# Half-matrix swaps by DMA alone: each engine's rows are regrouped from every sixteenth row to sixteen neighbouring rows, and half rows become whole rows in two pieces

## The chip, the cores and the metric

The kernel runs on one core of one Trainium2 chip. The metric is the device time of one execution in microseconds (us), lower is better. The computation uses no compute engine at all: everything is done by the core's 16 DMA engines, which copy from DRAM to DRAM.

## The reference

```python
x = np.random.randn(8192, 8192).astype(np.float32)

def reference(x):
    return np.fft.ifftshift(x)
```

For an even-sized matrix this exchanges the four quadrants diagonally: output row r, left half, is input row (r + 4096) mod 8192, right half, and output row r, right half, is the left half of that same input row. Each row is 32 KB, each half row 16 KB. The input holds 268.4 MB and so does the output; nothing is computed.

## The kernel before

Two engines issue DMAs, SyncE (`nc.sync`, SP in the profile) and ScalarE (`nc.scalar`, ACT in the profile); each has a DMA queue of its own, called q1 and q10 in the profile. Both queues feed the same 16 DMA engines.

`copy(queue, row, h, step)` at L25 to L32 issues one DMA of 256 half rows (4 MB) at L29. It fills the half of the output rows that starts at column `h` from the other half of the input rows that lie 4096 rows away. The list `dims` has three levels: 16 entries that are one row (32 KB) apart, then 16 entries that are 16 rows (512 KB) apart, then the 4096 neighbouring numbers of a half row. The outermost level is what the 16 DMA engines divide among themselves, so engine e takes rows e, e + 16, e + 32 and so on of the block of 256. At any one moment, if the engines keep step, they work on 16 neighbouring rows; call the number of the step within the DMA j (0 to 15), so that a row of the block is 16 j + e.

The loop at L36 to L39 walks over the output in groups of 1024 rows, four blocks of 256. SP takes the left output halves of blocks 0, 1, 2, 3 and ACT takes the right output halves of blocks 2, 3, 0, 1. That makes 64 DMAs, 32 on each queue. No DMA depends on another's data. The framework gives the DMAs eight completion semaphores in rotation, four for each queue, so each queue has four DMAs under way and its fifth waits for its first to land, and so on.

Of the kernel before, what the change touches and what calls it, by code (L numbers as in the profile page):

```python
# [1 line left out]

# [4 lines left out]


ENGINES = 16


@with_exitstack
def kernel(
    ctx: ExitStack,
    tc: tile.TileContext,
    x: bass.AP,
    out: bass.AP,
):
    nc = tc.nc
    R, C = x.shape  # L20
    hr = R // 2
    hc = C // 2
    per = 16
    rows = ENGINES * per

    def copy(queue, row, h, step):

        dims = [[C, ENGINES], [step * C, per], [1, hc]]
        queue.dma_start(  # L29
            out=bass.AP(out.tensor, out.offset + row * C + h, dims),  # L30
            in_=bass.AP(x.tensor, x.offset + (row + hr) % R * C + hc - h, dims),
        )  # L32

    for first in range(0, R, 4 * rows):  # L36
        for n in range(4):
            copy(nc.sync, first + n * rows, 0, ENGINES)
            copy(nc.scalar, first + (n + 2) % 4 * rows, hc, ENGINES)  # L39


# [1 line left out]
_INS = ['x']  # L43
_OUTS = [((8192, 8192), 'float32')]


def kernel(**inputs):
    import numpy as _np
    import concourse.bacc as _bacc
    import concourse.tile as _tile  # L50
    from concourse import mybir as _mybir
    from concourse.bass_utils import run_bass_kernel_spmd as _run

    nc = _bacc.Bacc("TRN2", target_bir_lowering=False, num_devices=1)  # L54
    arrays, args = {}, []
    for name in _INS:
        a = _np.ascontiguousarray(inputs[name])
        if a.dtype.kind in "iu":
            a = a.astype(_np.int64)
        arrays[f"in_{name}_dram"] = a  # L60
        args.append(nc.dram_tensor(f"in_{name}_dram", a.shape, _mybir.dt.from_np(a.dtype), kind="ExternalInput").ap())
    for i, (shape, dtype) in enumerate(_OUTS):
        dt = _mybir.dt.from_np(_np.dtype(dtype))
        args.append(nc.dram_tensor(f"out_{i}_dram", shape, dt, kind="ExternalOutput").ap())
    with _tile.TileContext(nc) as tc:
        kernel(tc, *args)
    r = _run(nc, [arrays], core_ids=[0])
    got = tuple(r.results[0][f"out_{i}_dram"] for i in range(len(_OUTS)))
    return got[0]
```

## Time and profile before

| quantity | value |
|---|---|
| median of 3 runs | 821.14 us (821.09 to 824.2) |
| span of the profiled execution, first to last instruction | 812.4 us |
| median less span (launch and end, outside the span) | 8.7 us |
| DMAs | 64 of 4096 KB, 32 on SP, 32 on ACT |
| DMA packets | 17408, of which 16384 carry 16 KB each and 1024 carry 4 bytes (completion counts) |
| bytes moved | 268.44 MB read and 268.44 MB written, 330 GB/s one way |

The page states no separate total for the profiled execution beside its span; the runs' times are about 8.7 us above the span. A packet is one contiguous piece moved by one DMA engine. "Landing" is the moment at which the last of a DMA's 16 completion counts arrives. A DMA share of 1.00 means that all 16 engines have a packet under way the whole time.

### The profile page before, as it was taken

What the parts mean: (1) busy time and instruction counts of PE and PEld (TensorE: products, weight loads), DVE (VectorE), ACT (ScalarE), POOL (GpSimd) and SP (SyncE); (2) the same over time, 40 slices, a digit from 0 to 9 for tenths busy, and PEclk for the clock granted to TensorE, in tenths of its full rate; (3) what the DMA queues carried; (4) which work ended last, traced back from release to release, by engine and by line L of the source; (5) the groups of instructions that cost most, each with busy time, mean ns of one, the idle gap of its engine ahead of it and who ended that gap; (6) DMA issues with size and microseconds to landing.
All of it is one profiled execution on the core that took longest, in us unless ns stands there. A gap on an engine that the chain in (4) does not pass through costs nothing. (4 is left out here: it accounts for less than half of the span.)

```text
span 812.4 us, 109 instructions
## 1 busy us (share of the span) xinstructions
POOL 0.2 (0%) x4
## 2 busy tenths in 40 slices
POOL 0000000000000000000000000000000000000000
DMA  9999999999999999999999999999999999999998
GB/s 307 331 331 336 335 331 331 335 325 337 334 332 336 331 333 332 334 339 332 332 334 331 329 331 334 332 328 333 330 334 335 334 328 333 332 331 330 338 331 280
DMA packets 17408, 268.44 MB, mean 330 GB/s; under 512 B 1024, under 2 KB 1024, under 8 KB 1024
## 3 DMA queue, kind: packets, MB, share of 16 engines
q1 hardware_dynamic: 8704, 134.22, 49.7%
q10 hardware_dynamic: 8704, 134.22, 49.5%
HBM read 268.44 MB, written 268.44 MB: 661 GB/s over the span
## 5 line engine op out<-in xcount | busy, mean ns | idle before, releaser
L54 POOL MEMSET const-bfloat16-1.0<- 128x1 bf16 x1 | 0.1, 101 | 0.0
L54 POOL MEMSET const-uint8-127<- 128x1 uint8 x1 | 0.1, 101 | 0.0
L54 POOL MEMSET const-float32-0.0<- 128x1 f32 x1 | 0.1, 98 | 0.2 <-issue 0.2
L54 POOL MEMSET const-float32-1.0<- 128x1 f32 x1 | 0.1, 98 | 0.0
## 6 DMA issues: line engine op xcount, KB each, us to landing
out_dram<-in_x_dram SPq DMA_DIRECT2D x32, 4096.0 KB, 101.0
out_dram<-in_x_dram ACTq DMA_DIRECT2D x32, 4096.0 KB, 101.0
```

The costliest lines, as they stand in the source:

```text
L54: nc = _bacc.Bacc("TRN2", target_bir_lowering=False, num_devices=1)
```

## The change

Each DMA now copies 256 whole rows (8 MB) in 16 KB pieces. The innermost two levels are the two halves of a row: on the input side the left half and then the right half, on the output side the right half and then the left half (the step of that level is negative). The outermost level has 256 entries, one row apart; divided among 16 DMA engines, engine e now takes rows 16 e to 16 e + 15 of the block, one after the other. The engines of one DMA are therefore 16 rows (512 KB) apart instead of one row (32 KB). SP takes the even blocks of 256 rows and ACT the odd ones; there are 32 DMAs instead of 64, 16 on each queue.

```diff
-    per = 16
-    rows = ENGINES * per
+    block = 256
 
-    def copy(queue, row, h, step):
-
-        dims = [[C, ENGINES], [step * C, per], [1, hc]]
+    def copy(queue, row):
+        src = x.offset + (row + hr) % R * C
+        dst = out.offset + row * C + hc
         queue.dma_start(
-            out=bass.AP(out.tensor, out.offset + row * C + h, dims),
-            in_=bass.AP(x.tensor, x.offset + (row + hr) % R * C + hc - h, dims),
+            out=bass.AP(out.tensor, dst, [[C, block], [-hc, 2], [1, hc]]),
+            in_=bass.AP(x.tensor, src, [[C, block], [hc, 2], [1, hc]]),
         )
 
-    for first in range(0, R, 4 * rows):
-        for n in range(4):
-            copy(nc.sync, first + n * rows, 0, ENGINES)
-            copy(nc.scalar, first + (n + 2) % 4 * rows, hc, ENGINES)
+    for first in range(0, R, 2 * block):
+        copy(nc.sync, first)
+        copy(nc.scalar, first + block)
```

## The prediction

> **What bounds the kernel now.** I read the page first. Nothing computes, so only its DMA parts matter.
>
> ```profile
> span 812.4 us, 109 instructions
> DMA  9999999999999999999999999999999999999998
> DMA packets 17408, 268.44 MB, mean 330 GB/s; under 512 B 1024, under 2 KB 1024, under 8 KB 1024
> q1 hardware_dynamic: 8704, 134.22, 49.7%
> q10 hardware_dynamic: 8704, 134.22, 49.5%
> HBM read 268.44 MB, written 268.44 MB: 661 GB/s over the span
> ```
>
> The two queues' packets fill 49.7 + 49.5 = 99.2% of 16 engines' time. There is no idle time to recover; a gain must make the pieces themselves shorter. Next, is the issuing of DMAs ever late? The waits of SP's queue, the timeline and the view of the output tensor say:
>
> ```profile
> SPq L29 <- DMA out_dram<-in_x_dram: 689.4, 28, 25.3
> 0.73 708.44 SPq L29 DMA_DIRECT2D out_dram<-in_x_dram  x32
> L29 SPq DMA_DIRECT2D out_dram<-in_x_dram x32: 571/571/652, 0.7 to 708.6; - x32
> DMA to landing us min/median/max: 25.6/101.0/103.4
> ```
>
> SP waits 28 times, that is for all but its first four DMAs, and issues each of the rest when the one four before it has landed. An issue takes 0.57 us and is followed by 101 us of queueing and moving, so four DMAs of 25 us each are always ready. Issue is not on the path. Last the windows view, for the ends:
>
> ```profile
> 0.00:5.00 5.00, 0.20 (x4) 1.00 0.61 210
> 100.00:200.00 100.00, 0.00 (x0) 1.00 1.00 332
> 806.00:809.00 3.00, 0.00 (x0) 1.00 0.95 317
> 809.00:812.40 3.40, 0.00 (x0) 1.00 0.06 24
> ```
>
> Its last two columns are the DMA share and GB/s. The middle is flat; start and end cost about 0.39 x 5.0 = 2.0 us and 0.05 x 3.0 + 0.94 x 3.4 = 3.3 us.
>
> So the time is the number of pieces per engine, 16384 / 16 = 1024, times the mean length of a piece. The trace holds each packet with its queue, start and duration; the mean over the 16384 pieces is 786.5 ns (lowest 608, a quarter of them at 611 or less, median 732, 95th percentile 1152). 1024 x 786.5 ns = 805.4 us; the span has 7.0 us more, of which start and end are 5.3. The median of the runs lies 8.7 us above the span: 805.4 + 7.0 + 8.7 = 821.1.
>
> A piece at 611 ns is 26.8 GB/s; five of the last pieces of all, when few engines are left, take exactly that. It is the pace of an engine that nobody disturbs. The other 175 ns of the mean is paid to the memory side. Hence the question is only whether the new order of addresses raises or lowers the 786.5.
>
> **Two facts from the packet records decide how I answer.** First, the engines keep step. The 16 completion counts of one DMA arrive within 1.1 to 2.8 us of each other in all 64 DMAs, though nothing in the program holds them together within the four DMAs under way. Second, pieces are not alike. I ordered each queue's pieces by start, cut them into DMAs (256) and steps (16), and averaged each step j over the 32 DMAs of the queue. Steps in fours, mean ns of a piece:
>
> ```
>             j 0-3    j 4-7    j 8-11   j 12-15
> q1          823.5    742.5    846.0    741.0
> q10         818.0    738.5    814.0    769.0
> ```
>
> Steps 0-3 and 8-11 (call their rows A) average 825.4 ns, the others (B) 747.8. The contrast holds in nearly every DMA (mean A less mean B is positive in 31 of 32 on q1 and 28 of 32 on q10). The queues are about three steps apart, so that one is often in A while the other is in B, and the A piece is still the longer one on its own engine. It goes with the piece's own rows, or with its place in its DMA, which here are the same thing: step j is always rows 16 j to 16 j + 15 of a block that starts at a multiple of 256 rows.
>
> **The change part by part.** Bytes, piece size (16 KB) and pieces per engine (1024) stay. Issues fall from 64 to 32: 32 x 0.57 us of queue time go, hidden before under 101 us of DMAs under way, so nothing comes off the time; four DMAs of 8 MB under way are about 202 us of cover. The 4-byte completion packets fall from 1024 to 512; they take 7 ns each, 32 fewer per engine are 0.2 us, which I drop. Left and right half of a row now follow each other on the same queue with one piece of the other queue between. No row of this trace shows such a pair; bounds are the two kinds of steps, 748 and 825 ns a piece (minus 40 to plus 40 us in all). I take zero, since 786.5 is a mean over many neighbourhoods of pieces and lies in the middle, and keep the ends for the range.
>
> The part that I think counts is the division. Before, every engine passed through A and B rows in turn, and so all were equal. After, engine e takes rows 16 e to 16 e + 15 of every block, which is what step j = e was: engines 0-3 and 8-11 get A rows for the whole run, engines 4-7 and 12-15 get B rows. If A rows are slow by their place in memory, the engines drift apart. A B engine ends its 1024 pieces after 1024 x 0.7478 = 765.7 us. By then an A engine has done 765.7 / 0.8254 = 928, and 96 are left. Then eight engines run alone. The low price for their pieces is 611 ns (58.7 us), the high one 825 ns (79.2 us); I take 640 ns, 61.4 us, near the floor, since eight engines at 26.8 GB/s ask for 215 GB/s where the memory side gave 332 all along. Sum: 765.7 + 61.4 + 7.0 + 8.7 = 842.8 us, with ends 840 and 861. The cover allows the drift: over 32 pieces on each of two queues a B engine gains 64 x 78 ns = 5.0 us, over the run 79 us, less than the 202 us of DMAs under way, so B engines needn't wait for A's.
>
> **The rivals.** (1) *No difference.* The contrast belongs to the place in the DMA (say, how descriptors reach an engine), not to the memory. Then every engine has the same mixture after, and the time stays at 821 us, 817 to 825. For it: the contrast has a period of eight steps through all DMAs, whatever the block's higher address bits. Against: queueing that starves an engine should show gaps between packets, and the packets fill 99.2%.
>
> (2) *Slower, and in step.* The engines are now 512 KB apart and keep step, as they did all along; then they lie in the same place of 16 different 512 KB stretches, and if these share banks, every piece pays at least the price of an A piece: 1024 x 0.8254 + 7.0 + 8.7 = 861 us; with the worst single step of the trace, 884 ns (q1, j = 9), 921 us. The same 861 comes out if the coupling that keeps the engines in step makes B engines wait for A's. It decides once the mean piece passes some 790 ns without one half of the engines ending early. For it: the tight step, and 175 ns of memory cost that can grow. Against: at distances of 32 KB the trace shows no such loss for any one engine. The Trainium skill, page "DMA: Bandwidth & Descriptors", section "Latency and other measured facts", has a row on row pitches at large powers of two: copies whose partitions lie 512 KiB apart ran at 207 GB/s per direction, where padded ones reached 214, and 2 MiB apart at 164. That speaks against this change; by 214 / 207 its time would be an estimated 849 us. No run here shows such a distance yet.
>
> (3) *Faster.* Reading a row's two halves one after the other, and spreading the 16 engines over 512 KB stretches, may break up what makes A steps slow, because they no longer meet 15 neighbouring rows of the same kind. If all pieces came at the B price: 1024 x 0.7478 + 7.0 + 8.7 = 781 us; half of that way 801 us. For it: 611 ns is possible and the mean lies 29% above it. Against: the 330 GB/s one way hardly moves in any slice of the run, as from a shared limit that doesn't care for order.
>
> (4) *It isn't what it says.* The compiler could join the two halves of the input row or divide the DMA otherwise. Pieces stay bound by the output side's 16 KB, so I'd expect about no change.
>
> **How the numbers follow.** Drift between A and B engines 0.34 (843 us); slower in step 0.23 (861, up to 921); faster 0.24 (801, down to 781); no difference 0.17, and not what it says 0.02 (821). A change within 0.5% (4 us) can't be told from none here, as the three runs lie 3 us apart. Faster by more: case 3 and a little of case 1, 0.25. Within: most of the cases at 821, 0.16. Slower: 0.59. The likeliest case's own range is 832 to 861, with its low end for a contrast of half the size. The range that holds 8 in 10 leaves out the lower half of case 3 and the upper part of case 2: 796 to 880.
>
> **What would show it.** In the profile after: 32 issues of 8192 KB and 16896 packets (16384 + 512); landing near 202 us. For drift: the 16 completion counts of one DMA spread by 5 us more with each pair of DMAs, to tens of us, while the middle stays at 332 GB/s, and the last 60 us fall to a DMA share near one half and about 215 GB/s. For case 1: spread of a few us and the same 332. For case 2: all slices lower, near 315, ends sharp. For case 3: all slices higher. A spread that stays under 5 us would prove the drift wrong.

## The result and the profile after

The changed kernel takes 872.34 us (median of 4 runs, 869.28 to 875.03) against 821.12 us (4 runs) for the kernel before on the same chip: 1.0617 times as long, 95% interval 1.0587 to 1.0647. The forecast was 843 us. The direction was right; the size was less than half of what came, and the mechanism was another.

The page of the changed kernel, the parts that answer to those shown of before:

```profile
span 868.0 us, 77 instructions
DMA  9999999999999999999999999999999999999998
GB/s 280 316 314 308 309 310 314 313 307 310 308 313 310 313 306 308 313 316 315 302 315 306 310 314 313 314 310 313 316 315 304 312 307 313 316 303 314 313 310 271
DMA packets 16896, 268.44 MB, mean 309 GB/s; under 512 B 512, under 2 KB 512, under 8 KB 512
q10 hardware_dynamic: 8448, 134.22, 49.8%
q1 hardware_dynamic: 8448, 134.22, 49.6%
HBM read 268.44 MB, written 268.44 MB: 618 GB/s over the span
```

The engines are as full as before (49.8 + 49.6 = 99.4%), the bytes are the same, and every one of the 40 slices is lower, 302 to 316 GB/s inside where before had 325 to 339; its line was:

```profile
GB/s 307 331 331 336 335 331 331 335 325 337 334 332 336 331 333 332 334 339 332 332 334 331 329 331 334 332 328 333 330 334 335 334 328 333 332 331 330 338 331 280
```

So each piece takes longer, evenly over the run: the mean of the 16384 pieces is 842.6 ns instead of 786.5. 1024 pieces an engine x 56.1 ns are 57.4 us; the span grew by 55.6 us. No stage and no wait holds the loss.

The waits of SP's queue, its row in the view of the output tensor, and that view's time to landing:

```profile
SPq L32 <- DMA out_dram<-in_x_dram: 140.6, 12, 53.9
L32 SPq DMA_DIRECT2D out_dram<-in_x_dram x16: 555/43842/50152, 0.7 to 648.1; - x16
DMA to landing us min/median/max: 54.1/215.7/218.3
```

An issue now takes a median of 43.8 us where it took 0.57, so there is a visible suspect: the queue seems no longer to accept four DMAs at once. Landing takes 215.7 us, still far more than an issue. The windows view, for the middle and the end (last columns: DMA share, GB/s):

```profile
100.00:200.00 100.00, 0.00 (x0) 1.00 1.00 311
780.00:800.00 20.00, 0.00 (x0) 1.00 1.00 311
860.00:864.00 4.00, 0.00 (x0) 1.00 0.97 295
864.00:868.00 4.00, 0.00 (x0) 1.00 0.45 147
```

The end is sharp: full until 4 us before it. There is no stretch of 60 us at half the engines. The 16 completion counts of each DMA arrive within 0.6 to 1.4 us of each other (before: 1.1 to 2.8). The drift that was forecast didn't happen.

### The profile page after: what moved, and what is told of

Read it like the earlier page. It is cut to its first block, busy times and chain, and to the rows that moved or that the text cites. A ratio compares the mean times of both kernels' runs of the same rounds, so it can differ in the third digit from the quotient of the medians.

```text
span 868.0 us, 77 instructions
## 1 busy us (share of the span) xinstructions
POOL 0.2 (0%) x4
## 2 busy tenths in 40 slices
DMA packets 16896, 268.44 MB, mean 309 GB/s; under 512 B 512, under 2 KB 512, under 8 KB 512
## 3 DMA queue, kind: packets, MB, share of 16 engines
q10 hardware_dynamic: 8448, 134.22, 49.8%
q1 hardware_dynamic: 8448, 134.22, 49.6%
## 6 DMA issues: line engine op xcount, KB each, us to landing
out_dram<-in_x_dram ACTq DMA_DIRECT2D x16, 8192.0 KB, 215.7
out_dram<-in_x_dram SPq DMA_DIRECT2D x16, 8192.0 KB, 215.7
```

## The experiments

Each ratio is to the kernel before on the same chip, with its 95% interval; the kernel before ran at 812.7 to 812.8 us in the first and the last group and at 822.4 to 822.8 us in the others.

**First group: the parts of the change one at a time.** Engines far apart, with all else as before:

```diff
-        dims = [[C, ENGINES], [step * C, per], [1, hc]]
+        dims = [[per * C, ENGINES], [C, per], [1, hc]]
```

> The kernel before (half rows, 64 DMAs of 4 MB, same blocks on the two queues), but each engine takes 16 neighbouring rows, so the engines are 512 KB apart instead of 32 KB. Theory D (distance between engines): about 872 us as in the changed kernel. Theory W (whole rows, left and right in turn on one queue): 821 us. Theory Q (8 MB DMAs, whose issue takes 44 us where it took 0.57 us): 821 us. Theory P (which blocks and halves the two queues work on at the same time): 821 us. If slow rows tied to engines matter by themselves, the 16 completion counts of one DMA spread by tens of us late in the run; if something holds the engines in step, by under 3 us.

Measured: 811.15 us, ratio 0.9985 (0.9963 to 1.0008), completion counts within 0.8 to 2.7 us. Read as it was meant, this acquits the distance; the last group shows that it had not tested it.

The pairing of the queues:

```diff
+    for first in range(0, R, 2 * rows):
+        for h in (hc, 0):
+            copy(nc.sync, first, h)
+            copy(nc.scalar, first + rows, h)
```

> The kernel before, except that SP takes both halves of the even blocks and ACT both halves of the odd ones, in separate 4 MB DMAs, so that both queues copy the same half of rows 256 rows apart at any time, as in the changed kernel. Theory P (pairing of the queues): about 872 us. Theories D, W and Q: 821 us.

Measured: 814.01 us, ratio 1.0011 (0.9987 to 1.0035). At 32 KB distance pairing costs nothing.

Whole rows with the engines near, by making the DMA small:

```diff
-    block = 256
+    block = 16
+    for first in range(0, R, 512):
+        for low in range(0, 256, block):
+            copy(nc.sync, first + low)
+            copy(nc.scalar, first + 256 + low)
```

> The changed kernel with DMAs of 16 rows (512 KB, 512 DMAs) instead of 256: one row an engine, so the engines are 32 KB apart as in the kernel before, while rows are still copied whole, left and right in turn. Theory D: about 821 us, perhaps a few us more for 512 issues. Theory W: 872 us. Theory Q: about 821 us.

Measured: 812.23 us, ratio 0.9996 (0.9978 to 1.0013). Left and right in turn costs nothing at 32 KB distance, nor do 512 issues.

Engines 17 rows apart (`[[C, 16 * 17], [-hc, 2], [1, hc]]`):

> The changed kernel with 17 neighbouring rows an engine instead of 16 (blocks of 272 rows, 30 of them, and two DMAs of 16 rows): the engines are 544 KB apart, which is no power of two. Theory D as a matter of powers of two: the loss goes, 815 to 830 us. Theory D as a matter of distance alone, theories W and Q: 865 to 880 us.

Measured: 841.15 us, ratio 1.0346 (1.0319 to 1.0373), between the two expectations. SP carried 53% of the bytes, so this was repeated evenly later.

**Second group: DMA size, the full queue, or distance and whole rows together (theory DW).**

```diff
f1:  block = 128
f2:  per = 32          # the kernel before, DMAs of 8 MB
f3:  little(queue)     # 16 numbers into SBUF after each big DMA
f4:  for low in range(16): ... [[16 * C, 16], [-hc, 2], [1, hc]]
```

> The changed kernel with DMAs of 128 whole rows (4 MB, 16 pieces an engine) instead of 256: 8 neighbouring rows an engine, engines 256 KB apart. Theory Q (a queue that holds more pieces than fit blocks the issuing engine, as the 44 us issues of the changed kernel show, and pieces then get slower): issues of about 0.6 us, four times 17 descriptors an engine under way as before, ratio to before 1.00. Theory DW (distance and whole rows are each harmless and bad together): ratio 1.04 to 1.06, or less if 256 KB is a better distance than 512 KB.

Measured: 823.09 us, ratio 1.0007 (0.9991 to 1.0023).

> The kernel before with 32 steps in a DMA instead of 16: half rows, engines 32 KB apart, 32 DMAs of 8 MB. Theory Q: issues of some 44 us and ratio 1.05 to 1.06 although order and distance are those of the kernel before. Theory DW: ratio 1.00.

Measured: 823.23 us, ratio 1.0005 (0.9983 to 1.0027).

> The changed kernel with two instead of four big DMAs under way on each queue: a DMA of 16 numbers into SBUF follows each big one and takes every second completion semaphore. Pieces, order and distances are those of the changed kernel, but only 66 descriptors an engine and queue are under way. Theory Q: issues under 1 us and ratio 1.00. Theory DW: ratio 1.06.

Measured: 868.64 us, ratio 1.0554 (1.0519 to 1.0589).

> The changed kernel's order of pieces and distance (whole rows, left and right in turn, engines 512 KB apart) in DMAs of 512 KB: one row of each engine in each. Theory DW: ratio 1.06. Theory Q: ratio 1.00, as the DMAs of 16 neighbouring rows had.

Measured: 872.15 us, ratio 1.0597 (1.0568 to 1.0626).

SP's rows in the view of the output tensor (minimum, median and maximum ns of an issue), of f2, f3 and f4 in this order:

```profile
L28 SPq DMA_DIRECT2D out_dram<-in_x_dram x16: 572/41472/48379, 0.7 to 616.8; - x16
```

```profile
L28 SPq DMA_DIRECT2D out_dram<-in_x_dram x16: 564/565/657, 0.7 to 757.6; - x16
```

```profile
L28 SPq DMA_DIRECT2D out_dram<-in_x_dram x256: 571/571/694, 0.7 to 855.9; - x128
```

This settles the suspect. f2 has issues of 41 us and loses nothing; f3 and f4 have issues of 0.57 us and lose 5.5% and 6.0%. Long issues come with four DMAs of 8 MB on a queue and cost nothing in f2. What the slow ones share is whole rows with engines 512 KB apart; f1, at 256 KB, is not slow. The cleanest pair is e2 and f4: both copy whole rows in 512 DMAs of 512 KB, one row of each engine in each, in blocks of 256 rows dealt to the queues in the same way. They differ only in which 16 rows a DMA takes, neighbours (e2, 0.9996) or rows 512 KB apart (f4, 1.0597).

**Third group: what goes with the distance.** Both queues on the same half, with half rows meant to be far apart; the queues on opposite halves; the queues 16 MB apart; and 1 MB between engines:

```diff
g1:  dims of e1_apart with the loop of e3_blocks
g2:  copy(nc.scalar, first + block, hc)       # ACT: right half of the input first
g3:  copy(nc.scalar, first + (n + 2) * block)
g4:  block = 512
```

> Half rows in 4 MB DMAs, engines 512 KB apart as in e1_apart, but with the blocks of e3_blocks: both queues copy the same half, 256 rows (8 MB) apart. Theory DP (distance and pairing: loss when the pieces of both queues sit at the same place of their 512 KB stretches): ratio 1.06. Theory DW (distance and left-right order within a queue): ratio 1.00.

Measured: 822.2 us, ratio 1.0000 (0.9979 to 1.0022).

> The changed kernel with ACT reading right, then left (and writing left, then right), so that the queues work on opposite halves while engines stay 512 KB apart and rows are whole. Theory DP with the half as part of the place: ratio 1.00. Theory DW: ratio 1.06. Theory DN (the loss needs the queues' blocks to be neighbours, 8 MB apart): ratio 1.06.

Measured: 859.39 us, ratio 1.0437 (1.0401 to 1.0474), 1.8 points less than the changed kernel. That doesn't show what opposite halves are worth, because the two queues came apart here. Their rows in the view of the output tensor:

```profile
L30 ACTq DMA_DIRECT2D out_dram<-in_x_dram x16: 660/47021/83707, 0.7 to 550.4; - x16
L30 SPq DMA_DIRECT2D out_dram<-in_x_dram x16: 554/554/1066, 0.7 to 773.5; - x16
```

ACT issued its last DMA at 550 us, SP at 774; ACT's last piece starts at about 771 us, and SP goes on alone to the end. While the queues still kept step, on opposite halves, the rate was 308 GB/s (10 to 110 us) and 313 GB/s (110 to 220 us); the changed kernel has 310 and 311 in the same stretches. So no gain shows in that part. The record of ACT's DMAs also has another shape, 1 x 512 pieces where SP's have 2 x 256, so that it isn't known which rows ACT's engines took.

> The changed kernel with the two queues 512 rows (16 MB) apart instead of 256, as in the kernel before. Theory DN: ratio 1.00. Theories DP and DW: ratio 1.06.

Measured: 870.79 us, ratio 1.0564 (1.0523 to 1.0606).

> The changed kernel in DMAs of 512 rows (16 MB): 32 neighbouring rows an engine, engines 1 MB apart, queues 16 MB apart. If distances that are larger powers of two are worse, as the step from 256 KB (1.00) to 512 KB (1.06) suggests: ratio 1.06 or more, up to 1.15. If 512 KB is a special distance: ratio near 1.00.

Measured: 1089.9 to 1165.0 us, ratio 1.3304 (1.3209 to 1.3398) from the lower two of its four runs, far above the 1.15 that was expected at most. The span and the GB/s of its page, which belongs to a run of 1134.0 us:

```profile
span 1132.2 us, 61 instructions
GB/s 223 236 246 242 233 235 240 244 241 237 234 240 239 242 230 237 234 240 238 237 231 234 238 239 245 237 241 239 242 239 227 238 241 235 238 236 243 239 243 212
```

With twice the distance the rate is about 240 GB/s all the way, 223 to 246 in all slices but the last. 256 KB, 512 KB, 1 MB give 1.00, 1.06, 1.33. Yet half rows at 512 KB seemed to lose nothing.

**Fourth group: the power of two, and why half rows escape.**

```diff
h1:  dims = [[32 * C, 16], [C, 32], [1, hc]]
h2:  dims = [[32 * C, 16], [2 * C, 16], [1, hc]]
h3:  block = 16 * 33     # whole rows; the rest of each half as one block of 16 * 25
h4:  block = 16 * 17     # whole rows; the rest as one block of 16 * 1
```

> Half rows, engines 1 MB apart, 32 neighbouring rows an engine in a DMA of 8 MB. Theory S (the loss goes by the number of pieces between one engine's rows and the next's: 16 pieces 1.00, 32 pieces 1.06, 64 pieces 1.33): 32 pieces, ratio 1.06. Theory I (half rows escape altogether): 1.00. Theory M (the distance decides, half rows only shift the point): over 1.06, up to 1.33.

Measured: 821.67 us, ratio 0.9992 (0.9968 to 1.0015).

> Half rows, engines 1 MB apart, every second row of an engine's 32 in one DMA of 4 MB and the others in the next, so that an engine steps 64 KB a piece. Theory S: 16 pieces, ratio 1.00. Theory I: 1.00. Theory M: as h1_half_1mb, over 1.06.

Measured: 823.31 us, ratio 1.0005 (0.9988 to 1.0021).

> Whole rows as in g4_block512, but 33 neighbouring rows an engine (7 blocks of 528 rows and one of 400 in each half of the matrix; both queues get the same share), so that engines are 1 MB and 32 KB apart. Power of two as the cause: from 1.33 to under 1.05. Distance as such, or number of pieces as such: 1.33.

Measured: 833.87 us, ratio 1.0126 (1.0098 to 1.0154).

> Whole rows with 17 rows an engine as in e5_seventeen, but with the blocks divided evenly over the queues (e5 gave SP 53%). Power of two as the cause: 1.00, e5's 1.035 having come from the uneven end. If the loss stays at 1.03 to 1.04, one row of stagger undoes only part of it at 512 KB.

Measured: 852.3 us, ratio 1.0350 (1.0318 to 1.0382), the same as e5's 1.0346, so the uneven queues hadn't mattered. The GB/s of h3's page, to be held against g4's:

```profile
GB/s 299 327 331 321 325 328 326 321 332 329 329 321 329 326 326 327 318 326 324 314 325 324 327 323 321 326 322 322 328 325 325 325 324 317 323 323 322 325 324 286
```

One row more in each engine's share, 33 instead of 32, and the rate goes from 240 to about 325 GB/s. At 1 MB, then, the loss goes with the power of two and not with distance as such. At 512 KB that is only half so: with 17 rows, 544 KB, one row of stagger takes away 2.7 of 6.2 points, and 3.5 stay.

h1 was too good, though: it doesn't only match the time of the kernel before. Mean ns of a piece by four steps, as in the prediction (h1 and f2 have 32 steps in a DMA), and the spread of the completion counts:

```
                 0-3    4-7   8-11  12-15  16-19  20-23  24-27  28-31   spread us
f2 (near)  q1   824.5  775.5  843.4  788.4  835.6  773.3  840.2  764.7   1.5-3.4
h1 ("far") q1   819.5  775.8  852.9  769.6  840.3  759.3  843.6  753.3   1.3-3.4
e3 (near)  q1   815.3  771.6  825.9  767.8                               1.1-4.1
g1 ("far") q1   822.0  777.9  868.3  770.3                               1.0-4.0
e1 ("far") q1   790.4  789.8  832.1  780.2                               0.8-2.7
f1 (whole) q1   795.3  799.0  804.0  805.1                               0.5-1.5
```

h1 and g1 bear the marks of their twins with near engines; in e1 the contrast is weaker than in the kernel before. And SP's issue rows in the view of the output tensor, first of the kernel before's pairing (e3), then of e1:

```profile
L28 SPq DMA_DIRECT2D out_dram<-in_x_dram x32: 571/571/726, 0.7 to 708.9; - x32
```

```profile
L28 SPq DMA_DIRECT2D out_dram<-in_x_dram x32: 511/511/609, 0.7 to 704.9; - x32
```

e1's issue is 60 ns shorter, because `[16 * C, 16], [C, 16]` is simply 256 rows in sequence: the two levels are joined, and the trace's record of the DMA says 256 x 1 pieces instead of 16 x 16.

**Last group: far half rows that can't be joined**, so that the levels stay 16 x 8 and 16 x 16:

```diff
i1:  dims = [[16 * C, 16], [C, 8], [1, hc]]     # two DMAs to a block
i2:  dims = [[32 * C, 16], [C, 16], [1, hc]]    # two DMAs to a block
```

> Half rows, engines 512 KB apart, 8 of an engine's 16 neighbouring rows in each DMA (2 MB), as 16 x 8 pieces that don't join into a flat list. Theory F (a flat list is dealt to the engines row by row, so e1_apart had its engines 32 KB apart; distance alone makes the loss, for half rows as for whole ones): ratio 1.04 to 1.08. Theory I (half rows immune): 1.00. Theory S (pieces between engines decide; here 16): 1.00.

Measured: 843.68 us, ratio 1.0394 (1.0360 to 1.0428).

> Half rows, engines 1 MB apart, 16 of an engine's 32 neighbouring rows in each DMA (4 MB), as 16 x 16 pieces. Theory F: ratio 1.2 to 1.4, as whole rows had at 1 MB (1.33). Theory I: 1.00. Theory S (32 pieces): 1.06.

Measured: 1038.5 us (1008.5 to 1061.4), 1.24 to 1.31 times the 812.7 us of the kernel before; no interval. The span and GB/s of its page, and SP's issue row:

```profile
span 1006.7 us, 109 instructions
GB/s 243 275 264 270 258 271 268 266 272 260 277 270 258 273 260 270 277 260 272 259 268 267 258 273 264 275 271 262 273 260 275 273 258 281 275 264 283 260 268 238
...
L29 SPq DMA_DIRECT2D out_dram<-in_x_dram x32: 571/572/666, 0.7 to 878.7; - x32
```

Half rows are not immune. With really distant engines they lose 4% at 512 KB and 24 to 31% at 1 MB. i1 and i2 differ from the kernel before in which rows the engines take; beside that i1 has DMAs of 2 MB, and in i2 the queues' blocks are 32 MB apart instead of 16 MB. That a joined list is dealt out row by row, so that engines were 32 KB apart in e1, g1 and h1 and 64 KB in h2, fits their times, but it is inferred; no record shows which engine moved which row. The shares of neighbouring rows in the changed kernel, i1 and i2 are inferred in the same way; f4, which names the 512 KB in its outermost level, takes as long as the changed kernel (1.0597 and 1.0617).

In i2 the steps have a strong rhythm. Mean ns of a piece by step, 0 to 15:

```
q1    797  765  853  916 1195  998 1145 1034   797  759  808  925 1040 1030 1115 1048
q10  1016 1123 1061 1092 1060  888  848  851   904 1096 1038 1094 1153 1020  901  863
```

It repeats every 8 rows, 256 KB, and goes from 759 ns, near a B piece of the kernel before, to 1195 ns. But the slow steps are 4 to 7 and 12 to 15 on q1, and 0 to 4 and 9 to 13 on q10. q10 runs about three steps behind: when q1 is in its slow steps 4 to 7, q10 is in its slow steps 1 to 4. Both queues are slow at the same moments and not at the same places, so a row's own place doesn't set the price.

**What holds.** When the engines advance in step, their distance sets the length of the pieces: nothing lost up to 256 KB (e2, f1), 4 to 6% at 512 KB (i1, f4, the change), 24 to 33% at 1 MB (i2, g4), and only 1.3% at 1 MB and 32 KB (h3). That is the change's loss, or most of it. Half rows lose about 2 points less at 512 KB (i1, 1.039) than whole rows (f4, 1.060); the two ran on different chips, and no run separates whole rows, left and right in turn, and equal halves on both queues at that distance, so these 2 points stay open. What in the memory makes such distances slow, no view shows. No version beat the kernel before.

## Why the prediction was right or wrong

**What bounds the kernel: right.** Full engines, time equal to pieces times mean length, and the mean length as the only thing that can move: 57.4 us from the pieces against 55.6 us of span.

**Issues and packets: right in cost.** 32 issues, 16896 packets, landing 215.7 us for 202 forecast. That issues would take 44 us wasn't foreseen; f2 and f3 show that it costs nothing. A completion packet takes 9 ns in the trace of the kernel before, not 7; 32 fewer of them on each engine are 0.3 us instead of 0.2, which changes nothing.

**Left and right in turn at zero: right for near engines** (e2, 0.9996). At 512 KB whole rows cost about 2 points more than the half rows of i1, and whether left and right in turn is the reason stays open.

**The division: the step that failed.** "Engines 0-3 and 8-11 get A rows for the whole run" was taken to mean that they go on paying 825.4 ns and the others 747.8. In place of these two terms all engines paid 842.6 ns and stayed within 1.4 us of each other; the tail of 61.4 us doesn't exist. That the time rose as forecast was therefore luck. The contrast was read as a property of rows. f1 speaks against that: if engines take neighbouring rows there as the code has it, engines 0-7 get A rows only and 8-15 B rows only, yet all stay within 1.5 us of each other and the mean piece is 796.9 ns, not 825.4. In i2 the same holds from the other side: the two queues are slow at the same moments, in different rows. The price goes with the set of addresses under way together.

**The rival that came true** is the second, slower and in step, which had 0.23. Its price, 861 us from 825.4 ns a piece, lay within 1.3% of the result, though that price was borrowed from A steps; the pieces measured 842.6 ns. That the engines stay in step and that distance makes the pieces longer is shown; the shared banks of its argument are not. The argument against it, that 32 KB distances show no loss, said nothing on 512 KB. The sign that should have weighed more was the tight step, with 0.3% between engines over the run (2.8 of 812 us): drift was forecast for engines that had shown they don't drift. Why they keep step stays open. The row of the Trainium skill, page "DMA: Bandwidth & Descriptors", section "Latency and other measured facts", pointed the right way: by it an estimated 849 us, 3.4% more; the runs have 3.9 to 6.2% at 512 KB. That row is about the pitch between partitions, and these runs about the distance between engines. At 1 MB between engines they show 24 to 33%.

**Rival 1** (the contrast belongs to the place in the DMA) is out as well: f1 has 16 steps in a DMA, and its four groups of steps on q1 lie between 795.3 and 805.1 ns, without the contrast. **Rival 3** (faster) never showed.

**The 8.7 us around the span** were mis-sized. After, the profiled execution took 869.81 us for a span of 868.0, 1.8 us more; all later pairs agree. So the profiled execution of the kernel before probably took some 814 us, 7 us less than its runs; groups of runs differ by 10 us as well. That is also why the spans lie 55.6 us apart and the medians 51.2.

## What to carry to other kernels

When engines keep step, ask which addresses are under way at the same moment, and keep the distance between them at 256 KB or less here, or off powers of two: one row in 33 gave back 32 of 33 points at 1 MB, but one in 17 only 2.7 of 6.2 at 512 KB. A contrast between steps measured under one access order is not a price list of addresses for another order. Before an experiment acquits a suspect, look for a sign that it did what its code says; here the DMA's recorded shape and the rhythm of piece lengths suggested that four kernels had not put the engines as far apart as their code says.

## What the runs showed that was not expected

- The same blocks of half rows cost 0.9985 in levels that join into one flat list (e1) and 1.039 as 16 shares of neighbouring rows that don't join (i1): how an access list is nested seems to decide which engine gets what.
- Issues of 41 us cost nothing in f2 (ratio 1.0005).
- At 1 MB distance the time also became uneven between runs, 1008 to 1061 us (i2) and 1090 to 1165 us (g4), where the kernel before stays within about 6 us on one chip.
